# First S5 layer of a four-layer trunk: in-projection in plain float32, tables ahead of the data, chunk states in column halves

## The chip, the cores and the metric

The kernel runs on one core of one Trainium2 chip. The metric is the time of one execution on the device in microseconds (us). The kernel before takes 1126.43 us in the median of 3 runs (1126.09 to 1129.15).

## The reference

A trunk of four layers, S5, HGRN2, attention with a window, S5, works on 512 tokens of width 1024 in float32. Every layer is one branch between two norms:

```
for i in range(DEPTH):                     # DEPTH = 4, mixer i % 3
    u = rms_norm(h, norm_pre[i])
    y = mixer(u, ...)                      # s5, hgrn2, attention, s5
    h = h + rms_norm(y, norm_post[i])

def s5_branch(h, ...):
    proj = h @ w_in                        # (512,1024) x (1024,2048)
    u, z = proj[..., :1024], proj[..., 1024:]
    # 64 groups of 16 channels, 64 complex states each
    # a = exp(lambda * dt), q = (a - 1) / lambda, b' = q * b
    # s[t] = a * s[t-1] + b' u[t]  (associative scan over 512 tokens)
    # y = Re(c s) + d * u
    y = gelu(y)
    y = y * sigmoid(y @ w_glu + b_glu)
    return (y * silu(z)) @ w_out
```

The change concerns the S5 branch, for the most part that of the first layer (layer 0).

## The kernel before, in words

**Projections.** Each is computed with float32 numbers cut in two parts (high and low, type fp32r) and three products instead of one: high weights by high x, high by low, low by high. A chunk of weights is 256 columns by 1024 rows, in two halves of 512 KB. SP loads the halves (tile `wraw`, L82 and 83, three buffers); `w_conv` writes the high part on ACT (`whi`, L105) and the low part on DVE (`wlo`, L106). `w_next` hands out a chunk, converts the next one and loads the one after. The three matmuls of a step stand at L139 (`ws`; output `pj`, 128 features by 256 or 512 tokens, eight steps of the contraction). The tokens come in by `norm_stats` and `norm_xt`: DVE scales x (L183), PE transposes it (`xtp`, L198), ACT writes `xh` (L202) and DVE `xl` (L203).

**A layer of S5.** `first_blocks` does the first four feature blocks (two chunks), in token halves of 256. Blocks 4 to 7 and then eight blocks of z follow with 512 tokens at a time. With eight steps of the contraction for each block that makes 64 steps of 256 tokens and 96 of 512, three matmuls each. Beside this run eight blocks of S5 proper. Once per layer `s5_tables` works out the powers of a (`ap`, `ea`, `eb`, many small instructions on DVE). For each block `s5_block_tables` makes `q` (L466, 468), `vt` (L476, 478), the taps `kps` (PE, L485), their transpose `ktp` (PE, L490), `ksb` (DVE, L494), eight copies from `ksb` to `toep` by SP's queue, the transposed `v` (`tps`, PE, L502) and `w` (L507, 509; its products t and t2w on POOL, L477, 508). For each pair of blocks `s5_rot` makes the phases (`rot`, L435 to 440, copied as `rotf` by SP). `s5_core` makes the chunk states `xps` (PE, L530), turns them by the phases (`xsw` on ACT, `xa` and `xsw` on DVE, L537 to 539), scans along the chunks (L541), turns back (`rsw`, `r`) and writes `spre` (DVE, L548); `yps` takes toep times u and w times spre (PE, L559, 561), ACT does the GELU, and for each pair of blocks PE transposes the output (`ytp`, L573). When all blocks are done `yh` (ACT, L614) and `yl` (DVE, L615) feed the GLU projection.

**What sets the order.** The program is written in the order of the functions above; a list scheduler then sets the order on each engine by its own idea of readiness and cost, and every engine executes its list in that order, one instruction after another. `behind` (`issue_after`) holds the instructions in its block behind a named one on each engine: in layer 0 `s5_open`, the tables and the tables of block 0 stand behind the statistics of x (`last_rstd`, `last_sq`), and the first conversion of weights behind the first scaled x (`first_xs`).

## Time and profile before

| | |
|---|---|
| median of 3 runs | 1126.43 us |
| profiled execution, its span | 1125.7 us (no other time of its own is recorded) |
| PE busy | 1032.6 us (92%) |
| DVE busy | 791.8 us (70%) |
| ACT busy | 522.5 us (46%) |
| POOL busy | 237.3 us (21%) |
| chain that ended last, by engine | PE 53%, DVE 27% |

The span runs from the first to the last event of the profiled execution and lies 0.7 us below the median of the runs. Layer 0 lies in the first 300 us or so, layer 3, the second S5 layer, behind 800 us. The shares are means over layers with different limits: in the fourth to seventh of the page's 40 slices DVE stands at nine tenths and PE at seven or eight.

### The profile page before, as it was taken

Reading aid. Unit: us, or ns where it says so; the run is one execution under the profiler, and the core shown is the slowest. Engines: PE = TensorE matmul, PEld = TensorE weight load, DVE = VectorE, ACT = ScalarE, POOL = GpSimd, SP = SyncE. Lnnn points to the kernel's source line nnn. Section 1 sums busy time; section 2 is a strip of 40 time slices with the busy share of each in tenths; the row PEclk is TensorE's granted clock in tenths of the full one; section 3 lists DMA queues with packets and bytes.
Section 4 is the critical chain, followed back from the end, with each engine's and each line's share of the span. In section 5 each row is a group of like instructions: output and inputs, shape, how many; then the busy total and the mean of one; then the engine's idle time right before and its main releaser. Section 6 shows DMA issues by size and latency. Waiting matters only on the chain.

```text
span 1125.7 us, 18462 instructions
## 1 busy us (share of the span) xinstructions
PE 1032.6 (92%) x7152; PEld 893.1 (79%) x7152; DVE 791.8 (70%) x1474; ACT 522.5 (46%) x1003; POOL 237.3 (21%) x218
## 2 busy tenths in 40 slices
...
GB/s 214 154 137 150 85 108 123 142 113 94 81 94 23 110 38 76 75 57 93 21 95 104 84 128 103 47 38 75 76 113 105 186 122 118 121 91 157 112 57 76
DMA packets 60327, 112.43 MB, mean 100 GB/s; under 512 B 23632, under 2 KB 33488, under 8 KB 59856
## 3 DMA queue, kind: packets, MB, share of 16 engines
...
## 4 chain that ended last, share of the span: by engine, by line
PE 53%; DVE 27%; issue 8%; ACT 4%; DMA 4%; POOL 3%; ACTq 1%; DVEq 0%; POOLq 0%; SPq 0%
PE pj L139 18%; PE ops L152 14%; PE zps L152 4%; DVE wlo L106 4%; PE vps L152 4%; PE sps L704 2%; PE scps L902 2%; DVE vt L476 2%; PE aops L938 2%; DVE xsw L538 2%; DMA rsw<-rraw 1%; PE ptp L933 1%; DVE sg L633 1%; DVE vt L478 1%; DMA rotf<-rot 1%
## 5 line engine op out<-in xcount | busy, mean ns | idle before, releaser
L139 PE MATMUL pj<-xh,whi 128*128 128x512 f32 (+1 forms) x656 | 235.8, 363 | 1.6 <-ACT whi L105 1.3
L139 PE MATMUL pj<-xl,whi 128*128 128x512 f32 (+1 forms) x656 | 234.4, 360 | 2.7 <-DVE xl L203 2.7
L139 PE MATMUL pj<-xh,wlo 128*128 128x512 f32 (+1 forms) x656 | 235.9, 361 | 0.1
L106 DVE TENSOR_TENSOR wlo<-wraw,whi 128x1024 fp32r<-128x1024 f32 x132 | 173.0, 1316 | 66.0 <-ACT whi L105 59.1
L105 ACT ACTIVATE whi<-wraw 128x1024 fp32r<-128x1024 f32 x132 | 138.4, 1054 | 63.6 <-PE pj L139 29.8
L152 PE MATMUL ops<-whi,gh 128*128 128x256 f32 x512 | 146.2, 286 | 2.1 <-ACT gh L635 1.7
L152 PE MATMUL ops<-whi,gl 128*128 128x256 f32 x512 | 144.7, 284 | 0.1
L152 PE MATMUL ops<-wlo,gh 128*128 128x256 f32 x512 | 144.6, 283 | 0.0
L139 PEld LDWEIGHTS pj<-xh,whi 128*128 128x128 f32 x656 | 126.4, 194 | 21.1 <-issue 5.1
L139 PEld LDWEIGHTS pj<-xl,whi 128*128 128x128 f32 x656 | 126.5, 193 | 19.9 <-issue 3.4
L139 PEld LDWEIGHTS pj<-xh,wlo 128*128 128x128 f32 x656 | 126.6, 193 | 18.6 <-issue 4.4
L152 PEld LDWEIGHTS ops<-whi,gh 128*128 128x128 f32 x512 | 97.9, 191 | 3.3 <-ACT gh L635 2.1
L152 PEld LDWEIGHTS ops<-whi,gl 128*128 128x128 f32 x512 | 97.6, 191 | 1.4 <-issue 1.0
L152 PEld LDWEIGHTS ops<-wlo,gh 128*128 128x128 f32 x512 | 97.8, 191 | 0.9 <-issue 0.8
L244 DVE TENSOR_TENSOR yg<-ops,gpost 128x256 f32<-128x256 f32 x64 | 26.9, 421 | 53.0 <-ACT junk L242 52.9
L242 ACT ACTIVATE junk<-ops 128x256 f32<-128x256 f32 x64 | 24.4, 381 | 72.4 <-PE ops L152 50.1
L162 POOL TENSOR_SCALAR rs_m<-po_st 128x1 f32<-128x1 f32 x16 | 3.1, 191 | 258.0 <-DVE po_st L248 258.0
L477 POOL TENSOR_TENSOR t<-ap,q 128x1024 f32<-128x1024 f32 x16 | 41.5, 2593 | 70.7 <-DVE ea L311 37.1
L162 POOL TENSOR_SCALAR rs_m<-hss 128x4 f32<-128x4 f32 x8 | 1.5, 194 | 246.4 <-DVE hss L762 246.4
L139 PE MATMUL pj<-yh,whi 128*128 128x512 f32 x128 | 48.9, 391 | 1.2 <-ACT yh L614 1.2
L508 POOL TENSOR_TENSOR t2w<-ap,prm 128x1024 f32<-128x1024 f32 x16 | 39.4, 2463 | 50.0 <-DVE vt L478 50.0
L139 PE MATMUL pj<-yl,whi 128*128 128x512 f32 x128 | 49.9, 391 | 0.0
...
## 6 DMA issues: line engine op xcount, KB each, us to landing
...
```

Of the source, the lines that this page charges most:

```text
L105: nc.scalar.activation(out=hi, in_=raw, func=AF.Copy)
L106: nc.vector.tensor_tensor(out=lo, in0=raw, in1=hi.bitcast(F32), op=ALU.subtract)
L139: self.nc.tensor.matmul(ps, lhsT=l[k // 4][:, k % 4, c], rhs=r[:, k, n0:n1], start=k == 0 and n == 0, stop=k == KB - 1 and n == 2)
L152: self.nc.tensor.matmul(ps, lhsT=l[:, k, c], rhs=r[k // 4][:, k % 4, :], start=k == 0 and n == 0, stop=k == KB - 1 and n == 2)
L242: nc.scalar.activation(out=junk, in_=ps, func=AF.Square, accum_out=ss[tb][:, c:c + 1])
L244: nc.vector.tensor_tensor(out=yg[:, tb, f], in0=ps, in1=gp[:, f], op=ALU.mult)
L476: nc.vector.tensor_tensor(out=vt, in0=bc(t["ap"][:, 0, gs, 0:8].unsqueeze(3), shp), in1=bc(q[:, 0].unsqueeze(2), shp), op=ALU.mult)
L477: nc.gpsimd.tensor_tensor(out=t2, in0=bc(t["ap"][:, 1, gs, 0:8].unsqueeze(3), shp), in1=bc(q[:, 1].unsqueeze(2), shp), op=ALU.mult)
L508: nc.gpsimd.tensor_tensor(out=t2, in0=bc(t["ap"][:, 1, gs, 1:9].unsqueeze(3), shp), in1=bc(s2.unsqueeze(2), shp), op=ALU.mult)
L538: nc.vector.tensor_tensor(out=xsw, in0=xsw, in1=sin, op=ALU.mult)
L704: nc.tensor.matmul(ps[:, c, :], lhsT=k[:, c * 128:c * 128 + 128], rhs=q4[:, c, :, 1, :], start=True, stop=True)
L902: nc.tensor.matmul(ps[:, bb, lo:256], lhsT=self.q[r, 4 * p + 2 * b2 + bb, qs], rhs=self.k[r, p, ks], start=True, stop=True)
```

## The change

Three edits, and the removal of all comments and docstrings.

1. The chunks of layer 0's in-projection are used as they were loaded: `plain(i)` names them, `w_load` puts the raw halves in the buffers that held `whi` and `wlo` (four each, so that up to four chunks are on hand, and `w_next` loads that far ahead), `w_conv` converts nothing, `norm_xt` writes one float32 x on ACT and nothing on DVE, and `ws` issues one float32 matmul in place of three fp32r ones.
2. `s5_open(0)` stands ahead of x and now holds only the clearing of some tiles; `s5_tables` and the tables of block 0 are no longer held behind the statistics of x in layer 0, and the hold of the first conversion goes.
3. In both S5 layers each matmul of `xps` becomes two, for columns 0 to 63 and 64 to 127 of `v`, with outputs on partitions 0 to 63 and 64 to 127.

```diff
@@ w_load
         for v in range(2):
-            raw = self.wpool.tile([P, 4, 256], F32, tag="wraw", name="wraw", bufs=3)
+            if self.plain(i):
+
+                raw = self.wpool.tile([P, 4, 256], F32, tag=("whi", "wlo")[v], name="wraw", bufs=4)
+            else:
+                raw = self.wpool.tile([P, 4, 256], F32, tag="wraw", name="wraw", bufs=3)
...
+    def plain(self, i):
+
+        return i < len(self.wseq) and self.wseq[i][:2] == ("s5_in", 0) and self.layers[0] == 0
+
     def w_conv(self, i):
         if i >= len(self.wseq) or i in self.wcv:
             return
+        if self.plain(i):
+            self.w_load(i)
+            self.wcv[i] = (self.wraw.pop(i), None)
+            return
...
-            with self.behind(self.first_xs if i == 0 else None):
-                nc.scalar.activation(out=hi, in_=raw, func=AF.Copy)
-                nc.vector.tensor_tensor(out=lo, in0=raw, in1=hi.bitcast(F32), op=ALU.subtract)
+            nc.scalar.activation(out=hi, in_=raw, func=AF.Copy)
+            nc.vector.tensor_tensor(out=lo, in0=raw, in1=hi.bitcast(F32), op=ALU.subtract)
@@ w_next
+        if self.plain(i):
+            for n in range(i + 2, i + 4):
+                if self.plain(n):
+                    self.w_load(n)
+            if self.plain(i + 1):
+                return self.wcv.pop(i)
@@ ws
+        terms = ((hi, xh), (hi, xl), (lo, xh)) if lo is not None else ((hi, xh),)
         for k in range(KB):
-            for n, (l, r) in enumerate(((hi, xh), (hi, xl), (lo, xh))):
-                self.nc.tensor.matmul(ps, lhsT=l[k // 4][:, k % 4, c], rhs=r[:, k, n0:n1], start=k == 0 and n == 0, stop=k == KB - 1 and n == 2)
+            for n, (l, r) in enumerate(terms):
+                self.nc.tensor.matmul(ps, lhsT=l[k // 4][:, k % 4, c], rhs=r[:, k, n0:n1], start=k == 0 and n == 0, stop=k == KB - 1 and n == len(terms) - 1)
@@ norm_stats, norm_xt
+            if self.plain(0) and L == 0:
+                self.x = (self.act.tile([P, KB, T], F32, tag="xh", name="xf"), None)
...
-                nc.vector.scalar_tensor_tensor(out=xl[:, k, c], in0=ps[:, kk, :], scalar=g, in1=xh[:, k, c].bitcast(F32), op0=ALU.mult, op1=ALU.subtract)
+                if xl is not None:
+                    nc.vector.scalar_tensor_tensor(out=xl[:, k, c], in0=ps[:, kk, :], scalar=g, in1=xh[:, k, c].bitcast(F32), op0=ALU.mult, op1=ALU.subtract)
@@ s5_core
         for g in range(8):
-            nc.tensor.matmul(xps[:, g, :], lhsT=t["v"][:, g, :], rhs=u[:, g, :], start=True, stop=True)
+            for o in (0, 64):
+                nc.tensor.matmul(xps[o:o + 64, g, :], lhsT=t["v"][:, g, o:o + 64], rhs=u[:, g, :], start=True, stop=True)
@@ layer_s5
-            with self.behind(self.last_rstd, self.last_sq if L == 0 else None):
-                self.s5_open(L)
+            with self.behind(self.last_rstd if L else None):
+                if L:
+                    self.s5_open(L)
+                self.s5_tables(j)
                 tabs = {0: self.s5_block_tables(j, 0)}
@@ trunk
+            if self.layers[0] == 0:
+                self.s5_open(0)
             x0 = self.act.tile([P, 4, D], F32, tag="y", name="x0")
```

(The memsets that `s5_open` now holds stood at the end of `s5_tables`.)

The scheduler sets the lists anew. In layers 1 and 2 they stay as they were; in layer 3 they change a little (one wlo fewer between its first vt and its last spre, and six in-projection matmuls behind its last yps in place of none). In layer 0 three places matter. `pj` are the in-projection's products, `xf` is the float32 x.

PE of layer 0, before, from the first block's transposes to the first xps:

```order
L490 MATMUL ktp<-cst,kt 128x128 x2
L502 MATMUL tps<-cst,vt 128x128 x4
L139 MATMUL pj<-xl,whi 128x512
L502 MATMUL tps<-cst,vt 128x128 x4
L139 MATMUL pj<-xh,wlo 128x512
L139 MATMUL pj<-xh,whi 128x512
L139 MATMUL pj<-xl,whi 128x512
L139 MATMUL pj<-xh,wlo 128x512
L530 MATMUL xps<-u,v 128x64 x8
```

PE of layer 0, after, from the end of the first four blocks (256 tokens wide) to the first xps:

```order
L157 MATMUL pj<-xf,wraw 128x256 x40
L507 MATMUL kps<-vt,c_85 32x128 x8
L157 MATMUL pj<-xf,wraw 128x512
L512 MATMUL ktp<-cst,kt 128x128 x2
L524 MATMUL tps<-cst,vt 128x128 x8
L157 MATMUL pj<-xf,wraw 128x512 x4
L507 MATMUL kps<-vt,c_91 32x128 x8
L157 MATMUL pj<-xf,wraw 128x512
L512 MATMUL ktp<-cst,kt 128x128 x2
L524 MATMUL tps<-cst,vt 128x128 x8
L157 MATMUL pj<-xf,wraw 128x512 x10
L553 MATMUL xps<-u,v 64x64 x16
```

Ahead of the first xps there were 57 fp32r matmuls of 512 tokens and one block's tables; now there are 16 float32 ones and the tables of two blocks.

PE at the end of layer 0's blocks, before, down to the last transposes of the output:

```order
L559 MATMUL yps<-toep,u 64x128 x2
L561 MATMUL yps<-w,spre 64x128 x2
L559 MATMUL yps<-toep,u 64x128 x2
L561 MATMUL yps<-w,spre 64x128 x2
L139 MATMUL pj<-yl,whi 128x512
L139 MATMUL pj<-yh,wlo 128x512
L139 MATMUL pj<-yh,whi 128x512
L139 MATMUL pj<-yl,whi 128x512
L573 MATMUL ytp<-cst,ysb 128x128 x8
L139 MATMUL pj<-yh,wlo 128x512
```

The same place after:

```order
L582 MATMUL yps<-toep,u 64x128 x2
L584 MATMUL yps<-w,spre 64x128 x2
L157 MATMUL pj<-xf,wraw 128x512
L596 MATMUL ytp<-cst,ysb 128x128 x8
L157 MATMUL pj<-xf,wraw 128x512 x23
L157 MATMUL pj<-yh,whi 128x512 x4
L157 MATMUL pj<-yl,whi 128x512
```

Before, the GLU's first seven products (`yh`, `yl`) stood ahead of the last yps and no product of z behind it; now 24 of z's 64 products stand behind the last yps and ahead of the GLU.

DVE in the middle of the blocks, before, between two chunk states (`spre` of one block, `xa` of the next):

```order
L548 TENSOR_TENSOR spre<-r,rsw 128x8x63
L440 TENSOR_TENSOR rot<-rot,rt 128x512
L468 TENSOR_TENSOR q_984<-q_984,q12b 128x256
L106 TENSOR_TENSOR wlo<-wraw,whi 128x1024
L476 TENSOR_TENSOR vt<-ap,q_984 128x1024
L507 TENSOR_TENSOR w<-ap,c_608 128x1024
L478 TENSOR_TENSOR vt<-vt,t_991 128x1024
L106 TENSOR_TENSOR wlo<-wraw,whi 128x1024
L537 TENSOR_TENSOR xa<-xps,rotf 128x512
L494 TENSOR_TENSOR ksb<-ktp,dmx 128x128
L538 TENSOR_TENSOR xsw<-xsw,rotf 128x512
```

The same stretch after, behind the spre of block 1:

```order
L571 TENSOR_TENSOR spre<-r,rsw 128x8x63
L500 TENSOR_TENSOR vt<-vt,t_794 128x1024
L529 TENSOR_TENSOR w<-ap,c_91 128x1024
L488 TENSOR_TENSOR q_930<-prm,co 128x256
L516 TENSOR_TENSOR ksb<-ktp,dmx 128x128
L490 TENSOR_TENSOR q_930<-q_930,q12b 128x256
L560 TENSOR_TENSOR xa<-xps,rotf 128x512
L561 TENSOR_TENSOR xsw<-xsw,rotf 128x512
```

The two wlo are gone from the stretch, and ksb stands ahead of xa, where it stood behind it.

## Rows read from the trace of the kernel before

**Rows 1.** Busy time by stretch: PE, PEld, DVE, ACT, POOL, clock, DMA share, GB/s.

```profile
17.00:75.20 58.20, 52.11 (x337) 46.31 (x337) 53.04 (x136) 26.90 (x51) 12.07 (x9) 0.97 0.58 157
75.20:201.10 125.90, 101.20 (x760) 79.40 (x760) 117.77 (x120) 63.26 (x101) 66.98 (x35) 0.97 0.43 114
201.10:250.40 49.30, 49.30 (x259) 41.44 (x257) 35.00 (x39) 28.48 (x41) 11.94 (x8) 1.00 0.39 122
885.00:1026.00 141.00, 114.70 (x849) 91.17 (x851) 131.73 (x131) 68.56 (x110) 74.77 (x41) 0.95 0.46 118
```

**Rows 2.** DVE in order of time: start, duration, instruction, idle before and its releaser.

```profile
75.22 0.68 DVE L537 TENSOR_TENSOR xa<-xps,rotf 128x512 f32<-128x512 f32 x1
77.93 0.29 DVE L494 TENSOR_TENSOR ksb<-ktp,dmx 128x128 f32<-128x128 f32 x1 [2.03 <-PE ktp L490]
...
147.93 3.38 DVE L106 TENSOR_TENSOR wlo<-wraw,whi 128x1024 fp32r<-128x1024 f32 x1
...
198.12 0.69 DVE L545 TENSOR_TENSOR r<-r,rotf 128x512 f32<-128x512 f32 x1 [1.40 <-ACT rsw L544]
...
200.42 0.68 DVE L548 TENSOR_TENSOR spre<-r,rsw 128x504 f32<-128x504 f32 x1
```

**Rows 3.** PE in order of time, end of layer 0's blocks.

```profile
199.84 1.20 PE L139 MATMUL pj<-yh,whi 128*128 128x512 f32 x4 [1.21 <-ACT yh L614]
...
204.37 1.04 PE L573 MATMUL ytp<-cst,ysb 128*128 128x128 f32 x8
205.16 0.47 PE L139 MATMUL pj<-yh,wlo 128*128 128x512 f32 x1
```

**Rows 4.** PE in order of time, from the first products of layer 0.

```profile
14.47 0.58 PE L139 MATMUL pj<-xh,whi 128*128 128x256 f32 x1 [1.25 <-ACT whi L105]
...
46.58 0.40 PE L139 MATMUL pj<-xh,whi 128*128 128x512 f32 x1
46.81 0.40 PE L139 MATMUL pj<-xl,whi 128*128 128x512 f32 x1
```

**Rows 5.** Groups on PE, whole run: count, busy, mean ns of one, idle before.

```profile
L139 PE MATMUL pj<-xh,whi 128*128 128x512 f32 x400 | 163.3, 408 | 0.3 <-ACT rraw L873 0.3
L938 PE MATMUL aops<-pt,av 128*64 128x512 f32 x56 | 20.5, 608 | 0.0
```

**Rows 6.** PE in order of time, yps of a late block of layer 0.

```profile
192.55 0.39 PE L559 MATMUL yps<-toep,u 128*64 128x128 f32 x4
192.77 0.39 PE L561 MATMUL yps<-w,spre 128*64 128x128 f32 x4
```

**Rows 7.** PE in order of time, block 0 of layer 0.

```profile
59.84 0.67 PE L485 MATMUL kps<-vt,c 128*32 128x128 f32 x16 [2.42 <-DVE vt L478]
...
65.66 1.89 PE L530 MATMUL xps<-u,v 128*128 128x64 f32 x16
67.36 0.48 PE L139 MATMUL pj<-xh,whi 128*128 128x512 f32 x1
```

**Rows 8.** PE in order of time, HGRN2 layer.

```profile
351.50 0.68 PE L722 MATMUL cps<-hqt,hk 128*64 128x64 f32 x8
```

**Rows 9.** Groups on DVE from 0 to 75.2 us.

```profile
L106 DVE TENSOR_TENSOR wlo<-wraw,whi 128x1024 fp32r<-128x1024 f32 x10 | 12.7, 1269 | 0.5 <-ACT whi L105 0.5
```

**Rows 10.** Groups on DVE from 75.2 to 201.1 us.

```profile
L106 DVE TENSOR_TENSOR wlo<-wraw,whi 128x1024 fp32r<-128x1024 f32 x9 | 14.8, 1648 | 0.2 <-ACT whi L105 0.2
L476 DVE TENSOR_TENSOR vt<-ap,q 128x1024 f32<-128x1024 f32 x6 | 14.2, 2374 | 0.0
L478 DVE TENSOR_TENSOR vt<-vt,t 128x1024 f32<-128x1024 f32 x7 | 8.5, 1214 | 1.9 <-POOL t L477 1.8
L466 DVE TENSOR_TENSOR q<-prm,co 128x256 f32<-128x256 f32 x6 | 4.1, 683 | 0.0
L435 DVE TENSOR_TENSOR rot<-ea,eb 128x512 f32<-128x512 f32 x3 | 2.2, 748 | 0.0
```

**Rows 11.** POOL in order of time.

```profile
147.54 2.68 POOL L509 TENSOR_TENSOR w<-w,t2w 128x1024 f32<-128x1024 f32 x1
```

41 lines of the change are left out of this document (20 added, 21 removed).

## The prediction

> **What bounds the kernel now.** I read the busy time by stretch first, since the shares of the whole span mix four layers. Layer 0 has two stretches before its GLU. From 17.0 to 75.2 us PE works 52.1 of 58.2 us and DVE 53.0: both are nearly full. From 75.2 to 201.1 us DVE works 117.8 of 125.9 us and PE 101.2 [rows 1]: DVE bounds, and PE has 24.7 us of slack. From 201.1 us the GLU keeps PE at 49.3 of 49.3 us, so whatever moves its start moves all that follows. Layer 3's blocks have DVE at 131.7 of 141.0 us.
>
> Next DVE in order of time. The second stretch begins with the first chunk state (xa) at 75.22 and ends with the last spre, 200.42 + 0.68 = 201.1 us. Its waits are few: 2.03 us of ksb for PE, 1.40 us of r for ACT's two rsw copies [rows 2].
>
> Last the end of the blocks on PE: the GLU's first product starts at 199.84 after a wait of 1.21 us for yh; eleven of its products stand ahead of the last transposes, which end at 205.16 [rows 3]. Without the yps and transposes between them the GLU would have begun at 205.16 - 11 x 0.23 = 202.6 us (0.23 us is the pace below). Against this I hold the changed kernel, in which everything else stands ahead of the GLU.
>
> **Plain float32 on PE.** fp32r products of 512 tokens start 0.23 us apart (46.58 to 46.81) [rows 4], so a step costs 0.69 us, one of 256 tokens half that, 0.345. No in-projection in plain float32 is in the trace. The nearest rows are the attention's: aops is plain float32, 512 wide, with two records for each matmul, and its mean is 608 ns where an fp32r record of that width shows 408 [rows 5]. A record thus takes 0.20 us longer than one at a pace of 0.23: 0.43, and a product 0.86 us. The other end comes from yps, plain too: two halves of 128 columns with two records each go by in 0.22 us [rows 6]; if the halves run side by side, 512 columns cost 0.88. I take 0.86, and 0.43 for 256 tokens. PE pays 64 x (0.43 - 0.345) + 96 x (0.86 - 0.69) = 5.4 + 16.3 = 21.7 us. Three matmuls become one, and still PE loses.
>
> **Column halves of xps.** Its 16 records take 65.66 to 67.36, 1.7 us [rows 7]. Of halves that are 64 columns wide with 64 to stream only a lone kind is in the trace, cps: eight records in 0.68 us, 0.085 each [rows 8]. In series 32 of them would take 2.7 us, side by side 1.4. The halves of yps, which stream twice as many columns, go by at 0.055 a record [rows 6], and with half the columns at 0.03: 0.9 us. Bounds 0.9 to 2.7; I take 1.0, next to yps, which also pairs its halves. PE saves 0.7 us x 8 = 5.6 us a layer. DVE covers most of it; it counts where DVE waits for PE, and if the bound is PE, it counts whole.
>
> The four records of yps begin within one 0.22 us and end by the next, two halves at a time [rows 6]. The Trainium skill ("TensorE: Matmul & The Clock Gate", part 3, The mechanism) speaks against the edit: a weight load overlaps matmuls in flight only when the row group differs, and the two halves differ in columns alone. By that the xps would take 2.7 us, 1.0 more than now, and the case of serial halves below gets its chance; by the rows of yps, whose halves also differ in columns alone, it does not hold here.
>
> **What leaves DVE and ACT.** 16 conversions on each and 24 xl on DVE. In the first stretch ten wlo (12.7 us) go [rows 9] and all xl, and since the tables start ahead of x, DVE is no longer late there; PE is. In the second stretch nine wlo become two. Their mean is 1.65 us there [rows 10] and 1.27 in the first stretch [rows 9]. I price seven at 1.27: 8.9 us. One vt (2.37 + 1.21) with its q (0.68) now stands ahead of the first xa: 4.3. So do two more of the rot products (0.75 each): 1.5 [rows 10]. Together 14.7 us.
>
> The wlo at 147.93 takes 3.38 us [rows 2] beside a POOL product that runs from 147.54 to 150.22 [rows 11]. The Trainium skill ("SBUF — State Buffer", Who interferes with whom) says that such a pair of operations takes turns on one shared port, the second blocked until the first is done; the row agrees, with the wlo's end 1.1 us behind POOL's. By that rule the wait passes to the next DVE instruction when a wlo goes; by the mean of 1.65, seven would give 11.5 us and the forecast 2.6 us less.
>
> **The first chunk state.** Products go from 14.47 to 46.58 before [rows 4], 32.1 us for 64 x 0.345 = 22.1; 10.0 us are transposes and waits for x and converted weights. After, 27.5 us of products, plus 0 to 10.0: they end between 42 and 52. Transposes and ACT's writing of x stay, the waits for xl and wlo go: I take 5.5, 47.5 us. Then by the order 16 products (13.8), two blocks' kps (0.67 each [rows 7]), ktp and tps (ten transposes at the 0.1 that the last eight take [rows 3], 1.0), a wait for the second block's vt like the 2.42 of kps now [rows 7], and xps: 13.8 + 3.4 + 2.4 + 1.0 = 20.6. First xa at 68.1 us, 7.1 earlier than 75.22.
>
> **The blocks.** DVE's 117.8 less 14.7 is 103.1 us. Its idle time: vt waits for POOL as now, 1.9 [rows 10], r for rsw 1.4 [rows 2]. New is ksb ahead of the third block's xa. Behind block 1's spre PE has its yps (eight times 0.22, 1.8), two products (1.7), the transposes (0.8), an xps (1.0), kps (0.7), one product (0.9) and ktp (0.2) to do, 7.1 in all, and ACT a copy (half of the 1.4 of two [rows 2], 0.7); DVE has vt, w (1.2 each) and q (0.7) to fill this with. ksb waits 7.8 - 3.1 = 4.7, and xa of the next block, long ready, is queued behind it. 1.9 + 1.4 + 4.7 = 8.0, so the stretch takes 111.1 us: last spre done at 179.2, 21.9 earlier.
>
> SP's queue: the last chunk's loads wait for a buffer that a product has to free, with two blocks' rotf copies behind them. The rotf are needed a whole block later; I cost this at nothing, and at up to 4.7 us (as ksb) if that cover fails.
>
> **The tail.** Behind the last spre stand the yps (1.8), one product (0.9), the transposes (0.8) and 23 products of z (19.8), then the wait for yh (1.2 as now): 24.5. The GLU starts at 203.7 us in place of 202.6: 1.1 late. What DVE gains PE's slower products take back, since they are no longer hidden but heaped up behind the last block. Break-even is a last spre at 178.1.
>
> **Layer 3.** One wlo fewer on the bounding DVE (-1.3), six products behind the last yps in place of none (6 x 0.23 = +1.4), shorter xps where DVE waits for one (0.7 each, once or twice within its idle 141.0 - 131.7 = 9.3: -1.1): -1.0, within -3.5 to +1.5. Layers 1 and 2: nothing.
>
> **Sum.** 1125.7 (the profiled span, 0.7 below the median of the runs) + 1.1 - 1.0 = 1125.8, with the 0.7 around it 1126.5 us. The terms' own bounds (first blocks' end within 42 to 52, but half of it covered by DVE's own chain; ksb 0 to 4.7; product 0.86 to 0.88) give 1121 to 1132.
>
> **Rivals.** PE becomes the only bound, without the stalls (faster). PE's work from 14.5 to 202.6 is 52.1 + 101.2 + about 2 at the two ends = 155; plus 21.7 less 5.6 is 171 us. With no idle time the GLU starts at 14.5 + 171 + 1.2 = 186.8, 15.8 early: 1110 at the extreme. For it: DVE needs only 103 us from 68 on, and PE products fill every gap. Against it: an in-order PE has 24 products left at the end, so it did wait before. Half-way gives 1112 to 1122, middle 1117.
>
> PE in order in grains of 0.86 us stalls DVE (slower). ksb's wait of 4.7 us, here counted once, recurs where ktp, xps or yps stand behind a run of 512-wide products; before, such runs had grains of 0.23 us that fell between. With two more blocks of the eight it is +9.4, with three +14.1: 1136 to 1140.6. For it: DVE already waited 2.03 us in just this place [rows 2]. Against it: later runs in the order are one to five products long. It decides from one further wait on (1131).
>
> The halves run in series: xps 2.7 us, 1.0 more on PE for each block, on DVE's path where it waits for xps: +1 to +8 in layer 0, +1 in layer 3, 1127 to 1135.
>
> **How the numbers follow.** Near break-even 0.45, PE alone 0.28, stalls 0.20, serial halves 0.07. 0.3% (3.4 us) is what can be told from no change: under 1123.0 is faster, above 1129.8 slower. Break-even gives 0.31 same and 0.07 on each side; PE alone 0.27 faster, 0.01 same; stalls 0.20 slower; serial halves 0.03 same, 0.04 slower. Sums: faster 0.34, same 0.35, slower 0.31. Range 1115 to 1137: it cuts off the extreme third of both far cases; the likeliest one's own is 1121 to 1132.
>
> **What would show it.** Products of 512 tokens in layer 0 0.86 us apart; xps of about 1.0 us; first xa near 68; last spre near 179; some 20 us of z products behind it with DVE idle; ksb of block 3 idle for some 5 us. Wrong if PE is without gaps from 50 us on and few z products remain (faster), or if DVE shows waits of several us for PE in more than one block (slower).

## The result and the profile after

The changed kernel takes 1155.99 us in the median of 4 runs (1153.88 to 1158.37), the kernel before beside it 1126.85: ratio 1.0251 [1.0233, 1.0270], slower by 29 us. The forecast was 1126.5, no change, with a range of 1115 to 1137. Sign and size lie outside it.

The profiled span is 1155.9 us against 1125.7, 30.2 more. Three marks divide this. The first out-projection of layer 0 starts at 267.2 in place of 246.3 (+20.9). The first `ut` of layer 3 starts at 887.7 in place of 866.2 (+21.5), so layers 1 and 2 add 0.6. From there to the end it takes 268.2 in place of 259.5 (+8.7). The loss thus lies in layer 0 and in layer 3.

The page after, busy time by engine and three rows of its slices:

```profile
PE 1059.7 (92%) x7248; PEld 871.1 (75%) x7248; DVE 743.7 (64%) x1434; ACT 507.6 (44%) x988; POOL 228.8 (20%) x218
...
PE   5688888999999999999999999999998887788997
...
DVE  6446897265666565665646556566568899995543
...
PEclk9889999999999999999999998999999989898999
```

A slice is 28.9 us, so layer 0 up to its out-projection takes the first nine. From the third to the seventh PE stands at 8 tenths, and DVE reaches nine tenths in one alone (the sixth); in the third (57.8 to 86.7) it is at 4. Neither engine is full there: each waits for something.

The stretches of layer 0 by busy time, in the columns of [rows 1], cut at the first kps, the first xa, the last spre, the GLU's first product and the first out-projection:

```profile
17.00:46.90 29.90, 29.90 (x151) 26.27 (x149) 25.70 (x86) 9.72 (x27) 7.41 (x5) 1.00 0.42 148
46.90:85.42 38.52, 24.55 (x141) 12.58 (x140) 12.28 (x13) 7.21 (x15) 13.00 (x9) 0.82 0.68 179
85.42:198.10 112.68, 94.36 (x719) 52.68 (x720) 91.99 (x102) 49.27 (x81) 49.23 (x29) 0.94 0.35 90
198.10:223.50 25.40, 24.23 (x87) 11.41 (x85) 2.31 (x3) 9.88 (x14) 3.06 (x2) 1.00 0.29 104
223.50:267.00 43.50, 43.47 (x192) 36.01 (x193) 27.87 (x37) 22.64 (x34) 9.30 (x6) 1.00 0.27 85
```

The second row is the failure that can be seen: 38.52 us in which PE works 24.55, DVE 12.28 and ACT 7.21, at a granted clock of 0.82. The forecast gave it 20.6. The third row answers to the 125.9 us of [rows 1]: 112.68, near the forecast of 111.1, but DVE works only 91.99 of it, not 103.

PE in order of time through the second row (start, duration, instruction, idle before and its releaser):

```profile
46.89 0.64 PE L507 MATMUL kps<-vt,c 128*32 128x128 f32 x16
47.47 1.12 PE L157 MATMUL pj<-xf,wraw 128*128 128x512 f32 x2
59.40 0.69 PE L512 MATMUL ktp<-cst,kt 128*128 128x128 f32 x2 [10.81 <-ACT kt L509]
59.88 1.92 PE L524 MATMUL tps<-cst,vt 128*128 128x128 f32 x8
61.59 5.41 PE L157 MATMUL pj<-xf,wraw 128*128 128x512 f32 x8
...
78.40 1.15 PE L553 MATMUL xps<-u,v 128*64 128x64 f32 x32
```

PE does one product (two records) after the first kps and stops for 10.81 us at `ktp`, which wants the copy `kt` of ACT. ACT in order of time:

```profile
45.27 0.41 ACTq L540 DMA_DIRECT2D ub<-ut  x1
57.48 0.33 ACTq L542 DMA_DIRECT2D u<-ub  x1
57.85 0.60 ACT L538 ACTIVATE ut<-pj 128x512 f32<-128x512 f32 x1 [12.62 <-DMA ub<-ut]
...
58.96 0.39 ACT L509 ACTIVATE kt<-kps 128x256 f32<-128x256 f32 x1 [0.51 <-ACT ut L538]
...
79.21 0.34 ACTq L483 DMA_DIRECT2D prm<-in_s_bc  x1
82.85 0.40 ACT L492 ACTIVATE c<-prm,cst 128x128 f32<-128x128 f32 x1 [10.58 <-DMA prm<-in_s_bc]
...
84.19 0.59 ACT L556 ACTIVATE xsw<-xps 64x512 f32<-64x512 f32 x1 [0.45 <-ACT ut L538]
```

ACT has little work and still holds everything up, since its list also issues DMAs. The load of `u` (L542) may be issued only when the write of `ub` has landed; until 57.48 it stands at the head of ACT's list. Behind it stand the next `ut`, whose only buffer that write is reading, and then `kt`. Later the load of `prm` stands at the head until its only buffer is free (79.21), and the copy `c` behind it until the load has landed (82.85). ACT's part of the first chunk state (`xsw`) waits behind both until 84.19, although xps is done at 79.4. DVE shows the stop at `ktp`, and an instruction of its own that waits for `prm` ahead of the first xa (`q`, L488):

```profile
60.12 0.29 DVE L516 TENSOR_TENSOR ksb<-ktp,dmx 128x128 f32<-128x128 f32 x1 [13.90 <-PE ktp L512]
...
82.85 0.43 DVE L488 TENSOR_TENSOR q<-prm,co 128x256 f32<-128x256 f32 x1 [5.68 <-DMA prm<-in_s_bc]
85.42 0.69 DVE L560 TENSOR_TENSOR xa<-xps,rotf 128x512 f32<-128x512 f32 x1 [2.14 <-ACT xsw L557]
```

What ran beside the slow write of `ub`: the DMAs issued from 45 to 58 us (tile, issuing queue, KB each, median us to landing), after:

```profile
DMA  2389999699699999999999999899999999999899
...
wraw<-in_s_in SPq DMA_DIRECT2D x4, 512.0 KB, 7.1
rotf<-rot SPq DMA_DIRECT2D x4, 256.0 KB, 8.5
ub<-ut ACTq DMA_DIRECT2D x1, 256.0 KB, 12.2
```

and before:

```profile
DMA  7999999998799799388959959944198999970000
...
ub<-ut ACTq DMA_DIRECT2D x2, 256.0 KB, 5.4
```

Since the tables are done ahead of x, SP issues four `rotf` and four halves of weights (3 MB) between 44.8 and 54.1 us, beside the one `ub`; before, it was three halves of weights (1.5 MB). How busy the DMA engines are does not tell the two apart: most slices of the DMA row stand at seven tenths or more in both. The Trainium skill ("DMA: Bandwidth & Descriptors", Issuing engines are not separate DMA queues) says that DMAs of all issuing engines run on the same 16 engines and interleave; 12.2 us against 5.4 agree. This profile is one execution; further ones below put the same write at 6.0 to 13.4.

### The profile page after: what moved, and what is told of

Same layout as the page of the kernel before. It is cut to its first block, busy times and chain, and to the rows that moved or that the text cites. A ratio compares the mean times of both kernels' runs of the same rounds, so it can differ in the third digit from the quotient of the medians.

```text
span 1155.9 us, 18574 instructions
## 1 busy us (share of the span) xinstructions
PE 1059.7 (92%) x7248; PEld 871.1 (75%) x7248; DVE 743.7 (64%) x1434; ACT 507.6 (44%) x988; POOL 228.8 (20%) x218
## 4 chain that ended last, share of the span: by engine, by line
PE 59%; DVE 20%; DMA 6%; issue 5%; ACT 4%; POOL 3%; ACTq 1%; DVEq 0%; SPq 0%; POOLq 0%
PE pj L157 24%; PE ops L170 13%; PE zps L170 4%; PE vps L170 3%; PE scps L927 2%; PE sps L729 2%; DVE vt L498 2%; PE aops L963 2%; DVE xsw L561 2%; DMA rsw<-rraw 1%; DMA prm<-in_s_bc 1%; DMA ub<-ut 1%; DVE vt L500 1%; POOL t2w L530 1%; DVE wlo L117 1%
## 5 line engine op out<-in xcount | busy, mean ns | idle before, releaser
L117 DVE TENSOR_TENSOR wlo<-wraw,whi 128x1024 fp32r<-128x1024 f32 x116 | 145.6, 1261 | 97.0 <-ACT whi L116 79.1
L157 PE MATMUL pj<-xh,whi 128*128 128x512 f32 (+1 forms) x496 | 179.2, 363 | 0.4 <-ACT rraw L898 0.4
L157 PE MATMUL pj<-xh,wlo 128*128 128x512 f32 (+1 forms) x496 | 178.2, 360 | 0.0
L157 PE MATMUL pj<-xl,whi 128*128 128x512 f32 (+1 forms) x496 | 177.2, 358 | 0.0
L116 ACT ACTIVATE whi<-wraw 128x1024 fp32r<-128x1024 f32 x116 | 121.6, 1055 | 64.0 <-PE pj L157 38.0
L157 PE MATMUL pj<-xf,wraw 128*128 128x512 f32 (+1 forms) x320 | 125.7, 537 | 0.0
L157 PEld LDWEIGHTS pj<-xh,whi 128*128 128x128 f32 x496 | 95.2, 193 | 16.4 <-issue 5.1
L157 PEld LDWEIGHTS pj<-xh,wlo 128*128 128x128 f32 x496 | 95.6, 193 | 14.3 <-issue 2.9
L157 PEld LDWEIGHTS pj<-xl,whi 128*128 128x128 f32 x496 | 95.7, 193 | 13.0 <-issue 2.2
L157 PEld LDWEIGHTS pj<-xf,wraw 128*128 128x128 f32 x320 | 59.6, 196 | 38.8 <-issue 34.5
L266 DVE TENSOR_TENSOR yg<-ops,gpost 128x256 f32<-128x256 f32 x64 | 26.9, 422 | 54.1 <-ACT junk L264 53.8
```

The source lines that it names most:

```text
L116: nc.scalar.activation(out=hi, in_=raw, func=AF.Copy)
L117: nc.vector.tensor_tensor(out=lo, in0=raw, in1=hi.bitcast(F32), op=ALU.subtract)
L157: self.nc.tensor.matmul(ps, lhsT=l[k // 4][:, k % 4, c], rhs=r[:, k, n0:n1], start=k == 0 and n == 0, stop=k == KB - 1 and n == len(terms) ...
L266: nc.vector.tensor_tensor(out=yg[:, tb, f], in0=ps, in1=gp[:, f], op=ALU.mult)
```

## The experiments

All ratios are to the kernel before on the same chip; the median of the runs stands beside them, in us (that of the kernel before is the one beside the changed kernel). The other columns come from the profiled run: start of the first xa and of the first out-projection of layer 0, PE's busy and idle time from 14.4 us to that out-projection (the first product starts between 12.8 and 16.6, so these two columns are good to 2 us), and the rest from there to the end, in us. A profile is one run: it was 5.2 us above the median in e5, 4.2 above in e15 and 3.3 in e14, 8.2 below in e12 and 3.9 in e8, and elsewhere within 2 us.

| kernel | median | ratio [95%] | xa | out-proj. | PE busy | PE idle | rest |
|---|---|---|---|---|---|---|---|
| before | 1126.85 | 1 | 75.2 | 246.3 | 199.1 | 32.8 | 879.4 |
| changed | 1155.99 | 1.0251 [1.0233, 1.0270] | 85.4 | 267.2 | 219.3 | 33.5 | 888.7 |
| e1 plain only | 1143.16 | 1.0137 [1.0121, 1.0152] | 76.8 | 261.0 | 219.7 | 26.9 | 880.8 |
| e2 tables only | 1135.27 | 1.0068 [1.0047, 1.0090] | 74.6 | 253.9 | 207.5 | 32.0 | 880.6 |
| e3 halves only | 1129.59 | 1.0014 [1.0001, 1.0028] | 76.8 | 246.9 | 199.8 | 32.7 | 881.9 |
| e4 changed in fp32r | 1136.39 | 1.0081 [1.0057, 1.0105] | 73.8 | 247.3 | 202.5 | 30.4 | 885.3 |
| e5 u on SP | 1150.84 | 1.0192 [1.0175, 1.0209] | 84.1 | 265.1 | 219.3 | 31.4 | 889.1 |
| e6 halves in layer 0 only | 1151.29 | 1.0200 [1.0178, 1.0222] | 87.1 | 271.4 | 222.8 | 34.2 | 879.1 |
| e7 z between blocks | 1153.04 | 1.0220 [1.0201, 1.0239] | 82.4 | 262.3 | 217.8 | 30.2 | 889.0 |
| e8 = e5 + e6 + e7 | 1147.32 | 1.0171 [1.0136, 1.0206] | 81.8 | 259.1 | 218.0 | 26.7 | 882.5 |
| e9 before, more PE | 1151.07 | 1.0202 [1.0184, 1.0221] | 72.3 | 269.0 | 227.7 | 26.9 | 880.8 |
| e10 changed, more DVE | 1151.00 | 1.0199 [1.0173, 1.0226] | 82.6 | 263.5 | 221.3 | 27.8 | 885.4 |
| e11 changed, half of z | 1129.09 | 1.0018 [0.9997, 1.0040] | 80.8 | 236.7 | 191.0 | 31.4 | 890.4 |
| e12 sz late | 1153.66 | 1.0215 [1.0178, 1.0252] | 81.4 | 261.3 | 217.1 | 29.8 | 882.4 |
| e13 kt, v on DVE | 1154.53 | 1.0239 [1.0206, 1.0273] | 83.3 | 262.7 | 216.2 | 32.1 | 888.8 |
| e14 = e13 + loads on SP | 1147.93 | 1.0185 [1.0158, 1.0213] | 84.6 | 261.6 | 217.3 | 29.9 | 887.8 |
| e15 all repairs | 1138.17 | 1.0102 [1.0073, 1.0130] | 84.2 | 257.3 | 216.9 | 26.0 | 883.2 |
| e16 loads held | 1154.58 | 1.0229 [1.0211, 1.0247] | 83.3 | 267.3 | 220.9 | 32.0 | 886.5 |
| e17 = e16 + e8 | 1147.77 | 1.0177 [1.0160, 1.0195] | 83.6 | 263.6 | 215.1 | 34.1 | 882.3 |
| e18 loads and prm held | 1146.98 | 1.0175 [1.0158, 1.0192] | 76.9 | 259.8 | 217.3 | 28.1 | 886.9 |

**The parts alone.** e1 takes the plain products and leaves xps whole and the tables where they were:

```
-            for o in (0, 64):
-                nc.tensor.matmul(xps[o:o + 64, g, :], lhsT=t["v"][:, g, o:o + 64], rhs=u[:, g, :], start=True, stop=True)
+            nc.tensor.matmul(xps[:, g, :], lhsT=t["v"][:, g, :], rhs=u[:, g, :], start=True, stop=True)
...
-            with self.behind(self.last_rstd if L else None):
+            with self.behind(self.last_rstd, self.last_sq if L == 0 else None):
+                self.s5_open(L)
```

> Of the three edits only the float32 in-projection; tables behind the data and whole xps as before. Queue theory (the loss comes from ACT, which stands at the issue of a u load until the slow ub write has landed, with kt and so PE behind it, and from a later yh in layer 3): the tables are late anyway, so the stop of PE behind kt is shorter than the 10.8 us of the changed kernel; layer 3's list on ACT has six yh ahead of the last GELU as before, so its 8 us do not appear: 1130 to 1140. Price theory (float32 costs PE 21.7 us and all of it shows; halves cost layer 3 the rest): 1126 + 21 = 1147.

e2 takes the early tables alone (`s5_open(0)` ahead of the data; the mark on the tables is gone, the hold of the first conversion stays):

```
-            with self.behind(self.last_rstd, self.last_sq if L == 0 else None):
-                self.s5_open(L)
+            with self.behind(self.last_rstd if L else None):
...
+            if self.layers[0] == 0:
+                self.s5_open(0)
```

> Of the three edits only the tables ahead of the data. Queue theory: fp32r loads are spread by three buffers, so the ub writes are not slowed; the first xa comes 0 to 4 us earlier: 1122 to 1127. Price theory: no price without float32, 1126 within 3. Shows whether the order with early tables alone sets the ACT queue against PE (then 1132 or more).

e3 takes the halves alone:

```
-            nc.tensor.matmul(xps[:, g, :], lhsT=t["v"][:, g, :], rhs=u[:, g, :], start=True, stop=True)
+            for o in (0, 64):
+                nc.tensor.matmul(xps[o:o + 64, g, :], lhsT=t["v"][:, g, o:o + 64], rhs=u[:, g, :], start=True, stop=True)
```

> Of the three edits only the column halves of xps, in both S5 layers. Queue theory: ACT's list at layer 3's end is as before (three yh ahead of the last GELU), PE has 5.6 us a layer less to do, mostly under DVE: 1124 to 1127. Price theory for layer 3 (the halves themselves cost it 8 us): 1134 or more.

e4 is the changed kernel with its products in fp32r as before:

```
-        return i < len(self.wseq) and self.wseq[i][:2] == ("s5_in", 0) and self.layers[0] == 0
+        return False
```

> The changed kernel with the in-projection of layer 0 put back to fp32r with high and low parts; tables ahead and halves stay. Queue theory: the 21 us of layer 0 go but for what early tables do to ACT's queue; layer 3 keeps its late order on ACT (eight yh behind the last z and a table load), +8: 1128 to 1137. Price theory: float32's 21 us go and nothing else is lost in layer 0: 1135. Apart by layer: first xa of layer 0 at 72 to 75 and start of the GLU at 202 to 203 by both; layer 3's tail +8 by the queue theory, by the price theory too if the halves do it, in which case the run with halves alone has them as well.

Each part is slower than before or level with it: 1143.16, 1135.27 and 1129.59 against 1128.18. Added up, they give 23.5 of the 29 us; layer 3 has most of the rest (below). Plain float32 is the largest part; e1 came out between its two expectations, e4 within both. Between e4 and the changed kernel it alone is the difference, and moves the out-projection from 247.3 to 267.2, by 19.9 of layer 0's 20.9: 16.8 us of PE's busy time and 3.1 of its idle time. The forecast had put the dearer products at 21.7: little of that was hidden.

The early tables cost 7 us by themselves, which neither theory had (it is the third case that e2's expectation names). PE has the same matmuls to do as before, and up to the out-projection it is busy for 207.5 us in place of 199.1, at a mean granted clock of 0.94 in place of 0.98.

The halves do what they should, and it does not show in the time. The groups of xps in layer 0 (count, busy, mean ns of one, idle before), of before:

```profile
L530 PE MATMUL xps<-u,v 128*128 128x64 f32 x128 | 16.1, 271 | 1.3 <-ACT v L503 1.2
```

and of e3:

```profile
L531 PE MATMUL xps<-u,v 128*64 128x64 f32 x256 | 11.7, 245 | 0.0
```

These are 4.4 us less, but PE's busy time to the out-projection stays (199.8 against 199.1), at a mean granted clock of 0.96 in place of 0.98: the time saved on xps came back as slower matmuls elsewhere. The whole kernel is level (1129.59), 2.6 us above what the queue theory gave.

**Is DVE the bound, with slack on PE?** e9 gives the kernel before 96 more products of 512 tokens in layer 0 (a doubled term, so that its output differs), 22 us of PE work that 24.7 us of slack would hide:

```
+            if self.wi <= 8 and n1 - n0 == T:
+                terms += ((hi, xh),)
```

> The kernel before with one more fp32r matmul in each of layer 0's 96 steps of 512 tokens (high by high a second time, so that u of blocks 4 to 7 and z are not the reference's): 96 x 0.23 = 22 us more on PE, about what plain float32 added, and nothing else. Slack theory (the prediction's premise: DVE bounds the blocks and hides PE's work up to PE's 25 us of slack): the time rises by less than 8 us. Price theory (PE's list keeps some 30 us of waits whatever is done, so PE's work shows whole): +17 to +22, with PE's idle time from its first product to the first out-projection still 27 to 34 us.

e10 gives the changed kernel 16 subtractions on DVE whose result nobody reads:

```
+            for raw in raws:
+                dead = self.wpool.tile([P, 4, 256], F32, tag="wraw", name="dead", bufs=3)
+                self.nc.vector.tensor_tensor(out=dead, in0=raw, in1=raw, op=ALU.subtract)
```

> The changed kernel with 16 subtractions of 128x1024 put back on DVE, one for each half of the weights, in the place of the wlo that went; nobody reads what they write. DVE gets 16 x 1.2 = 19 us more in layer 0. Slack theory (DVE sets the blocks): some ten of them fall behind the first xa, the time rises by 8 to 12 us. Price theory (PE sets the pace and DVE's relief was worth nothing): within 4 us of the changed kernel's 1156.

e11 takes half of z's products out of the changed kernel:

```
+        kb = KB // 2 if lo is None and self.wi > 4 else KB
-        for k in range(KB):
+        for k in range(kb):
```

> The changed kernel with half of the contraction left out in the z chunks of layer 0 (four of eight steps, z is not the reference's): 32 products fewer, 27.5 us less on PE. Price theory: PE's waits stay at 27 to 34 us, the GLU's end comes 22 to 28 us earlier, 1128 to 1134. Slack theory: the blocks keep their 113 us from the first xa, only the tail of 23 products goes: last spre at 198, 1134 to 1138. Apart by the last spre: earlier than 194 by the first, 196 to 200 by the second.

By the time of the whole kernel the three agree. Layer 0 by busy time, columns as above, of before:

```profile
14.40:246.30 231.90, 199.10 (x1320) 163.36 (x1321) 204.67 (x289) 116.46 (x191) 93.32 (x63) 0.98 0.46 127
```

of e9:

```profile
14.40:269.00 254.60, 227.73 (x1416) 187.96 (x1417) 200.56 (x290) 117.48 (x191) 87.14 (x58) 0.94 0.40 115
```

of the changed kernel:

```profile
14.40:267.20 252.80, 219.29 (x1295) 140.99 (x1294) 161.88 (x244) 100.98 (x176) 82.55 (x52) 0.95 0.40 114
```

of e10:

```profile
14.40:263.50 249.10, 221.28 (x1295) 143.97 (x1296) 187.71 (x260) 101.89 (x176) 80.92 (x52) 0.95 0.41 115
```

and of e11:

```profile
14.40:236.70 222.30, 190.95 (x1231) 130.52 (x1232) 168.00 (x242) 99.74 (x173) 81.08 (x52) 0.96 0.45 129
```

22 us more on PE make the kernel before 23.4 us slower (1151.07 against 1127.64), a little more than the price theory's 17 to 22. PE's idle time falls by 5.9 us, but its clock falls too, from 0.98 to 0.94, and its busy time rises by 28.6. 26 us more on DVE do not make the changed kernel slower: it is 5 us faster (1151.00), with a first xa 2.8 us earlier; why is open. 27.5 us less on PE make it 27 us faster (1129.09). So PE's time counts nearly one to one in both kernels, and DVE's did not count in the one where it was tried.

Where the time goes is not the same in the three. From the first xa to the end of the last spre (the blocks), and from there to the first out-projection, the profiles show, in us:

| kernel | blocks | PE busy in them | PE idle in them | DVE busy in them | behind them |
|---|---|---|---|---|---|
| before | 125.9 | 101.2 | 24.7 | 117.8 | 45.2 |
| e9 | 125.2 | 105.1 | 20.1 | 115.0 | 71.5 |
| changed | 112.7 | 94.4 | 18.3 | 92.0 | 69.1 |
| e10 | 111.6 | 95.9 | 15.7 | 99.6 | 69.2 |
| e11 | 115.6 | 92.4 | 23.2 | 101.3 | 40.3 |

In e10 only 7.6 of the 26 us fall into the blocks; they did not lengthen them. In e9 and e11 the blocks keep their length, and the difference stands behind the last block. By its own sign e11 therefore speaks for the slack theory: its last spre ends at 196.4, where that theory had 196 to 200 and the price theory less than 194. In e9 the last spre starts at 196.8 (before 200.4), and the GLU only at 225.3:

```profile
200.10 0.39 PE L564 MATMUL yps<-w,spre 128*64 128x128 f32 x4
...
225.27 1.21 PE L142 MATMUL pj<-yh,whi 128*128 128x512 f32 x4 [1.21 <-ACT yh L617]
```

The list placed most of the added products behind the last block, where they are bare. These two runs thus leave open whether PE's gaps inside the blocks could have taken them. e7, below, puts products there.

**The first stop.** e5 issues the load of `u` from SP in layer 0, so that ACT need not wait for `ub`:

```
-        nc.scalar.dma_start(out=u, in_=ub.rearrange("j (h g) c -> (j h) g c", g=8))
+        (nc.sync if self.s5L == 0 else nc.scalar).dma_start(out=u, in_=ub.rearrange("j (h g) c -> (j h) g c", g=8))
```

> The changed kernel with the u loads of layer 0 issued by SP in place of ACT, so that ACT no longer stands until a ub write has landed; PE's order around the first blocks is the same but for one product. Queue theory: PE's stop of 10.8 us before the first ktp and most of the slow clock behind it (3.4 us) go; the wait at the prm load stays. First xa at 70 to 74 in place of 85.4, DVE's stretch again 111 to 113, tail 25, GLU at 208 to 212 in place of 223.5: the time falls by 11 to 15, to 1141 to 1145. Rival (price theory: PE's added work is the bound, and its idle time in this layer is near 27 to 33 us in every order): the stop comes back as other waits, GLU at 219 or later, 1152 or more.

e13 makes `kt` and `v` on DVE in layer 0, past ACT's list:

```
+        if self.s5L == 0:
+            nc.vector.tensor_copy(out=kt, in_=kps)
...
+            if self.s5L == 0:
+                nc.vector.tensor_copy(out=v[:, 4 * hh:4 * hh + 4, :], in_=tps)
```

> The changed kernel with the copies kt and v of layer 0 on DVE in place of ACT (DVE has 90 us of idle time there, and PE stood 18 us for these two). New-wait theory (DVE's relief went into waits for ACT, whose list holds DMA issues that wait; PE's idle time is what these waits make it): PE's idle time from its first product to the first out-projection falls from 33.5 to 15 to 22 us, the time by 10 to 16, to 1140 to 1146. Rival (in this layer PE's list keeps 27 to 34 us of waits, whoever is waited for): idle 27 to 34, 1150 to 1157.

e14 adds that `u` and `prm` are loaded by SP in layer 0:

```
-        nc.scalar.dma_start(out=prm, in_=a["s5_bc"][j, b])
+        (nc.sync if self.s5L == 0 else nc.scalar).dma_start(out=prm, in_=a["s5_bc"][j, b])
```

> As the run with kt and v on DVE, and the loads of u and prm of layer 0 issued by SP, so that of layer 0's loads inside the blocks none waits at the head of ACT's list. New-wait theory: xsw follows xps at once, first xa at 72 to 76, PE idle 12 to 18, 1134 to 1142. Rival: the waits go to DVE (vt, spre, kt) or to SP's queue (u behind loads that wait for a buffer), idle 27 to 34, 1150 or more.

In e5 the stop at `ktp` falls from 10.8 to 1.8 us, but kps then waits 5.8 for ACT's `v` and `ktp` 4.9 in another block; the first xa gains 1.3. The load of `u` was not the only instruction to wait: the next `ut` stands in ACT's list for the same kind of write, with `v` behind it. ACT in e5:

```profile
60.05 0.60 ACT L538 ACTIVATE ut<-pj 128x512 f32<-128x512 f32 x1 [9.05 <-DMA ub<-ut]
```

The median of e5 (1150.84) lies between its two expectations. In e13 (1154.53, as its rival had it) the stop moves to DVE, whose `rot` waits until a copy of `rotf` has landed. PE's waits in layer 0 (who waits <- for whom: us, times, longest), e13:

```profile
PE kps L507 <- DVE vt L500: 14.1, 4, 10.6
PE ktp L515 <- DVE kt L510: 7.1, 4, 2.2
```

and DVE in e14:

```profile
59.70 0.69 DVE L443 TENSOR_TENSOR rot<-ea,eb 128x512 f32<-128x512 f32 x1 [10.24 <-DMA rotf<-rot]
```

In e14 (1147.93, between its expectations) DVE's `q` then waits for `prm` until 83.14, ahead of the first xa at 84.6. So taking ACT out of the way only shows the next one that waits for transfers. e16 goes to the transfers: the weights of chunks 4 to 7 are held behind block 1's copies to `toep`, and the calls that load two and three chunks ahead are taken out.

```
-            self.nc.sync.dma_start(out=raw, in_=self.a[name][j, c, v])
+            with self.behind(self.toepmark if self.plain(i) and i >= 4 else None):
+                self.nc.sync.dma_start(out=raw, in_=self.a[name][j, c, v])
```

> The changed kernel with the loads of layer 0's chunks 4 to 7 held on SP behind block 1's toep copies, so that they no longer run at 45 to 58 us beside the first ub and rotf. PE's order is the same but for one product. Burst theory (PE's first stop, for kt on ACT or for vt on DVE, is the same DMA burst seen from two sides): ub lands within 6 us instead of 12, PE's first stop falls from 10.8 to under 4, its idle time to 22 to 27, the time by 6 to 12, to 1144 to 1150. Rival (PE's list keeps its 27 to 34 us): another wait takes its place, 1151 or more.

e18 holds the load of `prm` behind the `xsw` of three blocks earlier as well:

```
-        nc.scalar.dma_start(out=prm, in_=a["s5_bc"][j, b])
+        with self.behind(self.xswmark.get((j, b - 3))):
+            nc.scalar.dma_start(out=prm, in_=a["s5_bc"][j, b])
```

> As the run with the loads of chunks 4 to 7 held, and on ACT each block's prm load from block 3 on held behind the xsw of the block three before, so that ACT no longer stands at that load with the first xsw behind it. PE's order is as in the run with the loads held, but for one product. First-state theory (given the first xa, the rest takes the same 181 to 184 us to the first out-projection in every version with this tail): first xa at 76 to 78 in place of 83.3, out-projection of layer 0 at 258 to 261 in place of 267, 1146 to 1149. Rival (waits only change places): first xa moves and the blocks grow by as much, 1152 to 1156.

In e16 the stop is 6.7 us, not under 4: the `u` load is issued 7.1 us after the write of `ub` (46.51 to 53.60) in place of 12.2. That does not show what the loads do. The changed kernel, e6, e7, e11 and e12 have the same lists up to there, without any hold, and in their profiles this write takes 6.0 to 13.4 us and the stop 4.3 to 12.3. The next write of `ub` tells more: it lands at 60.6 to 63.1 us in these five, and at 57.5 in e16 and e18. The first xps of e16 comes at 74.5 (from 78.4), but the held loads now go beside `prm` (issued at 74.51), `c` starts at 80.73, and the first xa comes at 83.3. The time (1154.58) is the rival's. With both held (e18) ACT reaches the first `xsw` at 75.68, directly behind xps:

```profile
75.68 0.59 ACT L557 ACTIVATE xsw<-xps 64x512 f32<-64x512 f32 x1 [0.49 <-PE xps L554]
76.29 0.59 ACT L558 ACTIVATE xsw<-xps 64x512 f32<-64x512 f32 x1
76.50 0.35 ACTq L482 DMA_DIRECT2D prm<-in_s_bc  x1
```

DVE's list changed with it: the `q` that waits for `prm` now stands behind the first xa. The first xa comes 8.5 us earlier than in the changed kernel, the out-projection 7.4, the median 9.0, all as the first-state theory had it. Against e16, which holds the same loads and has its first xps at the same time, it is 6.4, 7.5 and 7.6 us: the wait for `prm` costs that much. The hold of the loads alone brought 1.4 us in the median, that of `prm` alone was not tried. This part of the loss is shown, and it is less than a third of it.

**z, and layer 3.** e6 splits xps in layer 0 only:

```
-            for o in (0, 64):
+            for o in (0, 64) if self.s5L == 0 else (None,):
```

> The changed kernel with whole xps in layer 3; layer 0 keeps the halves. ACT's list at the end of layer 3 then has six yh ahead of the last GELU, where the changed kernel has all eight behind the last z, a table load and a sigmoid. Queue theory: the GLU of layer 3 starts 7 to 9 us earlier against the layer's start; 1147 to 1149. Rival (layer 3's loss comes with layer 0's delay, from weights or DMA): 1154 to 1157.

e12 puts z's sigmoid behind the last `yh` in ACT's list:

```
+                    with self.behind(self.last_yh):
                         nc.scalar.activation(out=sz, in_=self.z[:, k, :], func=AF.Sigmoid)
```

> The changed kernel with the sigmoids of z and their table load queued behind the last yh on ACT, in both S5 layers; halves everywhere. In layer 3 a table load (1.28 us) and a sigmoid (0.6) no longer stand between the last GELU and yh. If the late yh is what costs layer 3 its time: PE's wait for yh of 3.0 us falls to about 1, with it part of the slow clock behind it, layer 3 shorter by 2 to 5 us: 1151 to 1154. If the six products behind the last yps and the halves do it: no change, 1155 to 1157.

In e6 the rest after the out-projection is 879.1 us, before's 879.4: layer 3's loss is gone, so the halves there bring it, but not alone. From layer 3's first `ut` to the end it takes 259.5 us before, 259.8 to 261.6 in every other kernel with whole xps there, 261.5 in e3 with the halves alone, and 265.6 to 268.3 in every kernel with both the halves and the early tables, e4 without plain float32 included, but for e12. The edit of the tables touches layer 3's program as well (where the memsets stand); it takes the two together. (e6's time, 1151.29, still lies between its expectations. Its layer 0 came out 4.2 us longer in the profile, with a stop of 12.27 us; the same stop is 5.28 in e12, with the same lists up to there. What sets it is open.) The end of layer 3's blocks on ACT after:

```profile
1051.30 1.28 ACT L656 ACT_TABLE_LOAD   x1
1052.60 0.63 ACT L656 ACTIVATE sz<-z 128x512 f32<-128x512 f32 x1
...
1055.46 4.25 ACT L639 ACTIVATE yh<-y 128x512 fp32r<-128x512 f32 x8
```

and on PE after:

```profile
1052.71 0.39 PE L157 MATMUL pj<-xh,wlo 128*128 128x512 f32 x1
1056.12 0.80 PE L157 MATMUL pj<-yh,whi 128*128 128x512 f32 x1 [3.03 <-ACT yh L639]
1056.85 0.79 PE L157 MATMUL pj<-yl,whi 128*128 128x512 f32 x1
```

Before, ACT wrote the eight `yh` in three runs (1024.97, 1027.28 and 1030.29), the table load came behind the last at 1031.98, and PE passed from the last yps at 1026.33 to the GLU at 1026.68. Now the table load and a sigmoid stand ahead of all eight. PE stops for 3.03 us, and its next twelve matmuls go 0.43 us apart and more, where 0.23 is the pace elsewhere: the granted clock from 1056.1 to 1061.7 is 0.50, the lower of the two levels. The two together are 5.8 of layer 3's 8.7 us. The last yps itself starts 2.4 us later after the layer's first `ut`, and six products of z stand behind it. In e12's profile layer 3 takes 263.0 us, so 5.2 of the 8.7 are gone. That profile is of e12's fastest run (1145.50; the other three lie at 1153.49 to 1154.63), and its median (1153.66), as expected for a late yh, is only 2.3 below the changed kernel's.

e7 puts one of layer 0's chunks of z ahead of each of blocks 4 to 7, in place of all four behind the blocks:

```
+                if L == 0 and b in (4, 5, 6, 7):
+                    zchunk((4, 5, 6, 7).index(b))
```

> The changed kernel with layer 0's four z chunks written ahead of the cores of blocks 4 to 7 rather than behind all blocks, so that the list has no z product behind the last yps; the stop of PE at the first ktp stays. Tail theory (DVE sets the blocks, 113 us from the first xa, and the 23 products behind them are bare): first xa at 85, last spre at 198 to 205, GLU within 5 us of it, the time 13 to 20 lower: 1136 to 1143. Price theory (PE bound): the products only change place, the blocks grow by as much as the tail shrinks, 1152 to 1157.

e8 joins e5, e6 and e7:

> The changed kernel with all three: u loads of layer 0 on SP, z chunks between the blocks, whole xps in layer 3. If the three losses are separate, they add: 13 + 16 + 8 off 1156, 1115 to 1122, under the kernel before. If PE's work is the bound in layer 0 (171 us from 15.5 plus waits of some 20), the first two share one gain: 1130 to 1136.

e15 joins e14, e6 and e7:

> As the run before, with layer 0's z chunks between the blocks and whole xps in layer 3. New-wait theory: no tail, layer 3 as in the kernel before: 1124 to 1132, at best level with the kernel before, since PE's 16 to 20 us of float32 stay. Rival: 1143 to 1148, as the run with three repairs.

and e17 joins e16 and e8:

> Loads held as in the run before, with u on SP, z chunks between the blocks and whole xps in layer 3. Burst theory: 1147 of the run with three repairs less 6 to 10: 1130 to 1140, still above the kernel before, since float32's work on PE stays. Rival: 1143 to 1148 again.

In e7 the tail is short, but the blocks grew. From the first xa to the last spre (columns as in [rows 1]):

```profile
82.43:225.25 142.82, 124.28 (x809) 70.13 (x809) 97.88 (x111) 58.48 (x94) 48.23 (x29) 0.94 0.31 78
```

Against the changed kernel's 112.7 us they take 30.1 more; PE works 29.9 more in them, and its idle time stays at 18.5 (18.3). Behind them it is 37.1 in place of 69.1, the out-projection comes 4.9 us earlier, and the time is 1153.04, as the price theory had it. So products put between the blocks cost nearly what they cost behind them. (They stand there in runs of eight; a finer mixture was not tried.)

e8 (1147.32) is slower than both of its expectations: the three gains do not add. e15 is the best changed version, 1138.17, between its expectations and still above the kernel before (1.0102 [1.0073, 1.0130]); it has the least idle PE (26.0) of all. e17 (1147.77, its rival's range) gains nothing over e8. No version beat the kernel before.

## Why the prediction was wrong

**What held.** A plain product takes 0.858 us for 512 tokens (0.86 foreseen). xps in halves takes 78.40 to 79.39, 0.99 us (1.0): the forecast's case of serial halves is refuted, and the rule of the Trainium skill ("TensorE: Matmul & The Clock Gate", part 3, The mechanism) that would have made it 2.7 does not hold for these halves. The first blocks end at 46.9 (47.5). From the last spre's end to the GLU it is 25.4 us (24.5). From the first xa to the last spre's end it is 112.7 (111.1), but by luck, since two errors cancel. DVE's work is 11 us less than the 103.1 foreseen: the first operation of vt takes 1.56 us on average in place of 2.37, for example. Its idle time is 20.7 in place of 8.0: it waits 7.6 for `prm`, which the forecast did not have, and 4.1 in place of 1.4 for ACT's `rsw`.

**Where the sum went wrong.** Against the kernel before, the first xa was to come 7.1 us earlier and came 10.2 later. The blocks were to be 14.8 shorter and are 13.2 shorter. The tail of z, foreseen at 24.5, is 25.4. Of the 19.8 us by which the GLU misses the forecast (223.5 for 203.7), 17.3 are the first xa, 1.6 the blocks and 0.9 the tail. (In the five profiles with the same lists up to the stop, the first xa lies between 80.8 and 87.1.)

**The term "First xa at 68.1".** This is the step that failed. Of the 20.6 us from the first kps, 38.5 were measured, 17.9 more. The stop at `ktp` adds 10.8. Products, kps and transposes take 3.5 more, most of it from 59.4 to 66.9 us, where the granted clock is 0.61. From the end of xps to xa it is 6.0, of which 4.8 are the wait behind `prm` and 1.2 the two `xsw` copies, for which the sum has no term. The wait of 2.4 for vt did not come. The reason lies in what the forecast says of SP's queue, "I cost this at nothing": what SP issues was weighed only against the buffers that it waits for, not against the `ub` that goes beside it. ACT's list, on which `kt` and `xsw` stand behind DMA issues and what waits for them, got no term at all. e18 shows the part that can be taken away: 8.5 us of the first xa and 7.4 of the out-projection. A stop of 6.5 us at `ktp` is left in it.

**The premise: "DVE bounds, and PE has 24.7 us of slack".** This failed too. It read the idle time of PE in the stretch of [rows 1] as room for more work. In e7 PE's gaps took up none of the 29.9 us that were put between the blocks, and in e9, where most of the 22 us came to stand behind the blocks, they cost 23.4. In e10 7.6 us more of DVE in the blocks did not lengthen them. PE executes its list in order, and it idled in given places, for given results: PE's waits of layer 0, before, were first of all

```profile
PE kps L485 <- DVE vt L478: 13.3, 7, 3.0
PE yps L561 <- DVE spre L548: 10.0, 5, 3.2
```

and after

```profile
PE ktp L512 <- ACT kt L509: 15.4, 3, 10.8
PE kps L507 <- ACT y L597: 6.1, 2, 3.2
PE yps L584 <- DVE spre L571: 4.7, 4, 1.5
```

DVE's relief did come (the two waits for it fall from 23.3 us to 4.7 and 2.1), and waits for ACT took their place. PE's idle time is 26.0 to 34.2 us in all twenty kernels, whether DVE works 160 or 205 us, and so the out-projection moves as PE's busy time does: 20.2 of the 20.9 us are busy time. The forecast's own sum of PE work was +21.7 - 5.6 = 16.1. It was to be paid for by the earlier first xa and the shorter blocks. Measured are 20.2 more, at a granted clock of 0.95 in layer 0 in place of 0.98.

**Layer 3, "-1.0, within -3.5 to +1.5".** It was +8.7. e6 shows that it is not there without the halves in layer 3, and e2, e3 and e4 that it takes the halves and the edit of the tables together. With both, a table load and a sigmoid stand ahead of all `yh` in ACT's list; e12's profile puts 5.2 us on that, and the rest was not taken apart. The six products behind the last yps were in the forecast. It counted the work of the engines and not the order of ACT's list.

**The rivals.** PE as the only bound, "without the stalls", was nearer right about what counts and wrong in dropping the stalls. PE in order in grains of 0.86 us was right that the kernel gets slower. But what was to show it, DVE waiting for PE in several blocks, did not: between the first xa and the last spre it waits once, 2.6 us at ksb. Its price was too small as well. Each held one half.

**What stays open.** Why PE's idle time stays near 30 us whatever is moved is seen, not explained: the releasers change from kernel to kernel, and the list scheduler reorders with each edit. The 8.8 us by which the first xa of e18 still misses the forecast were not tried any further. The stop at `ktp` scatters from 4.3 to 12.3 us between executions with the same lists up to there, so single profiles in the table are good to some us only, and how much of the stop is due to the loads beside `ub` was not shown. Why the granted clock of layer 0 is lower in e2, e3 and the changed kernel was not taken apart, nor why more work on DVE made e10 faster.
